# Loading the first two batches of a batched matmul one by one, with one load issued by a second engine

## The chip, the cores and the metric

The kernel runs on one core of a Trainium2 chip. The metric is device time in microseconds (us), of which the median of several executions is quoted. A profile also gives a *span*, from the first to the last recorded instruction. The span of this kernel is some 2 us shorter than its time.

## The reference

Sixteen independent products of 512 x 512 matrices in float32, with the left one transposed:

```python
a: (16, 512, 512) float32   # batch, k, m
b: (16, 512, 512) float32   # batch, k, n
out = np.matmul(a.transpose(0, 2, 1), b).astype(np.float32)
```

That is 33.55 MB to read and 16.78 MB to write.

## The kernel before

Batches are taken in eight pairs. One DMA loads both batches of a pair of `a` (2 MB), another those of `b`: batch 0 of the pair lies in partitions 0 to 63, batch 1 in 64 to 127, and each partition gets one contiguous run of 8 rows, 16 KB. There are four such float32 buffers. VectorE casts to bf16 in two halves (`v`), TensorE multiplies (two 64-row matmuls side by side, one for each batch), ScalarE copies PSUM to an output tile, and SyncE issues the DMAs. It issues all sixteen loads first and then the stores, which so stand behind the loads on one queue.

```python
for n in range(2 * pairs):                      # 16 loads, a and b in turn
    if n >= NX:                                 # NX = 4 buffers
        nc.sync.wait_ge(s_in, n - NX + 1)       # casts of load n - 4 done
    nc.sync.dma_start(x_ts[n % NX][:], in_v[n % 2][n // 2]).then_inc(s_x[n % NX], 16)
for i in range(pairs - 1):                      # the stores follow on the same queue
    nc.sync.wait_ge(s_out, i + 1)
    nc.sync.dma_start(out_v[i], o_ts[i % NO][:]).then_inc(s_o if i else s_o0, 16)
...
for i in range(pairs):                          # VectorE
    for v in range(V):
        if i and v == 0:
            nc.vector.wait_ge(s_v, G * i)
        if i and v == 1:
            nc.vector.wait_ge(s_mm, G * H * i)
        for n in (2 * i, 2 * i + 1):
            if v == 0:
                nc.vector.wait_ge(s_x[n % NX], 16 * (n // NX + 1))
            nc.vector.tensor_copy(...).then_inc(s_cast, 1)
            if v == V - 1:
                nc.vector.memset(dve_done[:, n:n + 1], 0.0).then_inc(s_in, 1)
```

## Time and profile before

| | before |
|---|---|
| time, median | 123.92 us (123.84 to 124.15, 4 runs) |
| span of the profile | 121.9 us |
| DMA engines busy | 97.6% |
| busiest compute engine | TensorE, 51% |
| DMA rate from 4 to 79 us (loads) | 430 to 434 GB/s |
| first cast, first matmul | 8.84 us, 15.19 us |

Each load and store ends with one small semaphore write on each of the 16 DMA engines, and the trace records them. The mean of the sixteen is called the *end* of a load in what follows. In the kernel before, ends in the middle of the run are 4.86 us apart.

### The profile page before, as it was taken

The page shows a single profiled execution, that of the slowest core. Times are in us where ns is not written, and L with a number is a line of the kernel's source. Part 1 is how long each engine was busy: PE and PEld are TensorE (multiplying, and loading weights), DVE is VectorE, ACT ScalarE, POOL GpSimd, SP SyncE. Part 2 cuts the span into 40 slices and gives each one's busy share as a digit, 9 for nine tenths or more (in the row PEclk, how much of TensorE's full clock was granted, in tenths as well). Part 3 has the DMA queues.
Part 4 walks back from the last instruction along what each step waited for, and adds up shares of the span by engine and source line. Part 5 has one row for each costly group of instructions (what it writes and reads, how often), then busy time and mean ns, then how long its engine had stood idle before and what let it go on. Part 6 is the DMA issues. An engine that isn't in the chain of part 4 may idle for free. (4 is left out here: it accounts for less than half of the span.)

```text
span 121.9 us, 1261 instructions
## 1 busy us (share of the span) xinstructions
PE 62.5 (51%) x512; PEld 35.8 (29%) x512; DVE 38.0 (31%) x48; ACT 31.8 (26%) x41; POOL 0.2 (0%) x4
## 2 busy tenths in 40 slices
PE   0000099989669749969919988946960000000000
PEld 0000044546246314536605645624630000000000
DVE  0003560784194092474356247419000000000000
ACT  4000000480920830190470075091083000000000
POOL 0000000000000000000000000000000000000000
PEclk9999999999999977999995899999999655555555
DMA  5899999999999999999999999999999999999994
GB/s 108 360 430 430 436 430 430 430 430 430 430 430 430 430 430 436 430 430 430 430 430 430 430 430 430 436 390 428 428 430 430 430 428 430 430 430 428 428 428 175
DMA packets 4480, 50.33 MB, mean 413 GB/s; under 512 B 384, under 2 KB 384, under 8 KB 384
## 3 DMA queue, kind: packets, MB, share of 16 engines
q1 hardware_dynamic: 4480, 50.33, 97.6%
HBM read 33.55 MB, written 16.78 MB: 413 GB/s over the span
## 5 line engine op out<-in xcount | busy, mean ns | idle before, releaser
L103 PE MATMUL ps<-bbf,abf 64*128 64x512 bf16 x512 | 62.5, 403 | 27.9 <-PEq L98 27.9
L103 PEld LDWEIGHTS ps<-bbf,abf 64*128 64x128 bf16 x512 | 35.8, 114 | 54.1 <-issue 37.8
L121 ACT COPY o<-ps 128x1024 f32<-128x1024 f32 x32 | 30.1, 1026 | 59.8 <-PE ps L103 59.8
L82 DVE CAST abf<-x 128x2048 bf16<-128x2048 f32 x16 | 19.6, 1224 | 26.6 <-PE ps L103 17.6
L82 DVE CAST bbf<-x 128x2048 bf16<-128x2048 f32 x16 | 19.6, 1225 | 20.8 <-DMA x<-in_b_dram 20.8
L126 ACT ACTIVATE done<-done 1x1 uint32<-1x1 uint32 x8 | 1.6, 196 | 0.0
L121 ACT ACT_TABLE_LOAD x1 | 1.3, 1283 | 0.9 <-SPq L64 0.9
L88 DVE MEMSET done<- 1x1 f32 x16 | 0.9, 59 | 0.0
L148 POOL MEMSET const-bfloat16-1.0<- 128x1 bf16 x1 | 0.1, 101 | 0.0
L148 POOL MEMSET const-uint8-127<- 128x1 uint8 x1 | 0.1, 101 | 0.0
L148 POOL MEMSET const-float32-0.0<- 128x1 f32 x1 | 0.1, 98 | 0.2 <-issue 0.2
L148 POOL MEMSET const-float32-1.0<- 128x1 f32 x1 | 0.1, 98 | 0.0
## 6 DMA issues: line engine op xcount, KB each, us to landing
x<-in_a_dram SPq DMA_DIRECT2D x8, 2048.0 KB, 12.1
x<-in_b_dram SPq DMA_DIRECT2D x8, 2048.0 KB, 15.9
out_dram<-o SPq DMA_DIRECT2D x8, 2048.0 KB, 30.8
```

What stands on the lines that cost most here:

```text
L82: nc.vector.tensor_copy(out=(bbf_ts if n % 2 else abf_ts)[v][:], in_=x_ts[n % NX][:, v * RV:(v + 1) * RV, :],).then_inc(s_cast, 1)
L88: nc.vector.memset(dve_done[:, n:n + 1], 0.0).then_inc(s_in, 1)
L103: mm = nc.tensor.matmul(ps_ts[g][h][:, t % 2, :], a_m[:, t], bbf_ts[v][rows, r, :], start=(v == 0 and r == 0), stop=(v == V - 1 and r == R ...
L121: ev = nc.scalar.copy(out=o_ts[i % NO][:, g, 2 * h:2 * h + 2, :], in_=ps_ts[g][h][:])
L126: nc.scalar.memzero(act_done[:, i:i + 1]).then_inc(s_out, 1)
L148: nc = _bacc.Bacc("TRN2", target_bir_lowering=False, num_devices=1)
```

## The change

First a and first b of pair 0 are loaded batch by batch, so that batch 0 (1 MB of `a`, 1 MB of `b`) is complete after half the bytes. Its `b` is issued by ScalarE at the same time as its `a` by SyncE. The aim is to let TensorE start earlier. Each partition then holds four rows of one batch (8 KB runs), and this pair uses 128-row matmuls. Both batches go through the same bf16 tiles, so VectorE must wait for the matmuls of batch 0 before it casts batch 1.

```diff
+    in0_v = [x.rearrange("batch (p r) m -> batch p r m", r=RV) for x in (a, b)]
...
-        for n in range(2 * pairs):
+        for u in range(G):
+            for j in range(2):
+                (nc.sync if u or j == 0 else nc.scalar).dma_start(
+                    x_ts[j][:, u * RV:(u + 1) * RV, :], in0_v[j][u]
+                ).then_inc(s_x[j] if u else s_f[j], 16)
+        for n in range(2, 2 * pairs):
...
+        for u in range(G):
+            if u:
+                nc.vector.wait_ge(s_mm, H)
+            for j, bf_ts in enumerate((abf_ts, bbf_ts)):
+                nc.vector.wait_ge(s_x[j] if u else s_f[j], 16)
+                nc.vector.tensor_copy(
+                    out=bf_ts[0][:], in_=x_ts[j][:, u * RV:(u + 1) * RV, :]
+                ).then_inc(s_cast, 1)
+                if u == G - 1:
+                    nc.vector.memset(dve_done[:, j:j + 1], 0.0).then_inc(s_in, 1)
... (VectorE: the old loop from pair 1 on, where pair 1 waits for all matmuls of pair 0;
     TensorE: a loop of two batches with 16 128-row matmuls each, then the old loop for 7 pairs;
     ScalarE: the four copies of pair 0 in batch order)
```

## The prediction

> **What bounds the kernel now.** I read the page first, parts 1 to 4, for which engine is full and when; then the stretches table, to find where the full resource is not full; then the timeline of the start and the queue's own waits, because that is where the change acts.
>
> ```profile
> PE 62.5 (51%) x512; PEld 35.8 (29%) x512; DVE 38.0 (31%) x48; ACT 31.8 (26%) x41; POOL 0.2 (0%) x4
> DMA  5899999999999999999999999999999999999994
> q1 hardware_dynamic: 4480, 50.33, 97.6%
> HBM read 33.55 MB, written 16.78 MB: 413 GB/s over the span
> ```
>
> No compute engine is above 51% of the span, while the 16 DMA engines are 97.6% busy and show a 9 in all but the first two slices and the last. The kernel is bound by moving 50.33 MB. The chain of work that ended last covers only 7% of the span for the same reason: it ends at the issue of the last store, and nearly everything else is transfers, which the chain does not price. What the change can win is therefore only DMA time that is not used at full rate. The stretches table says where that is (last two columns: DMA share and GB/s).
>
> ```profile
> 0.00:2.00 2.00, 0.00 (x0) 0.00 (x0) 0.00 (x0) 1.10 (x1) 0.20 (x4) 1.00 0.12 33
> 2.00:4.00 2.00, 0.00 (x0) 0.00 (x0) 0.00 (x0) 0.18 (x1) 0.00 (x0) 1.00 0.94 229
> 4.00:6.00 2.00, 0.00 (x0) 0.00 (x0) 0.00 (x0) 0.00 (x0) 0.00 (x0) 1.00 1.01 434
> 6.00:15.00 9.00, 0.00 (x0) 0.00 (x0) 2.56 (x3) 0.00 (x0) 0.00 (x0) 1.00 1.00 430
> 15.00:60.00 45.00, 38.35 (x312) 21.43 (x314) 22.44 (x29) 15.81 (x21) 0.00 (x0) 0.96 1.01 431
> 79.00:82.00 3.00, 1.64 (x16) 0.79 (x12) 0.21 (x1) 3.00 (x4) 0.00 (x0) 1.00 0.93 380
> 90.00:120.00 30.00, 0.42 (x4) 0.00 (x0) 0.00 (x0) 2.58 (x4) 0.00 (x0) 0.59 1.01 427
> 120.00:121.90 1.90, 0.00 (x0) 0.00 (x0) 0.00 (x0) 0.00 (x0) 0.00 (x0) 0.50 0.07 26
> ```
>
> From 4 us to 120 us the rate is 427 to 434 GB/s, except for a dip where loads give way to stores. Against 431, the deficits are 1.85 us in the first row (2.00 x (1 - 33/431)), 0.94 us in the second, 0.35 us at 79 to 82, and about 1.8 us at the end. These add up to 4.9 us, and 50.33 MB at 431 GB/s is 116.8 us; together 121.7 of the span's 121.9. Only the second row, 0.94 us, is something this change can act on: the first is the time before the first DMA can be issued and reach the engines, the last is the end of the program.
>
> The start itself, by the timeline:
>
> ```profile
> 0.94 0.39 SPq L68 DMA_DIRECT2D x<-in_a_dram  x1
> 1.39 0.42 SPq L68 DMA_DIRECT2D x<-in_b_dram  x1
> 8.84 1.23 DVE L82 CAST abf<-x 128x2048 bf16<-128x2048 f32 x1 [8.84 <-DMA x<-in_a_dram]
> 13.67 1.23 DVE L82 CAST bbf<-x 128x2048 bf16<-128x2048 f32 x1 [3.60 <-DMA x<-in_b_dram]
> 15.19 9.54 PE L103 MATMUL ps<-bbf,abf 64*128 64x512 bf16 x64 [15.19 <-PEq L98]
> 16.08 0.33 SPq L68 DMA_DIRECT2D x<-in_a_dram  x1
> 17.23 0.33 SPq L68 DMA_DIRECT2D x<-in_b_dram  x1
> 23.44 1.23 DVE L82 CAST bbf<-x 128x2048 bf16<-128x2048 f32 x1 [0.87 <-DMA x<-in_b_dram]
> ```
>
> The first a (2 MB) lands at 8.84, the first b at 13.67, TensorE starts at 15.19. That idle start looks like a loss, and it is what the change attacks. But the fifth load, the first that waits for a buffer, is issued at 16.08, and the last of the four loads before it lands at 23.44: the queue holds over 7 us of work when it gets more. Late compute never starves the transfers.
>
> **What the Trainium skill says.** "DMA: Bandwidth & Descriptors", section "Issuing engines are not separate DMA queues", says that DMAs from scalar, sync or gpsimd run on the same 16 engines and interleave, so issuing from several saves only the sequencer's issue time. The trace before uses one queue and cannot show the interleaving; it does show the issue time at stake, 0.39 to 0.42 us per load, against some 4.9 us for which a load keeps the engines busy. The same page, section "Queues, rings and completion order", says that each engine goes round-robin between the queues it has work for, packet by packet: so first a and first b should land together. No run here shows that yet. Section "Where 436 GB/s comes from" puts the ceiling at 435.2 GB/s; the trace agrees, with 427 to 434 in every full stretch, so there is no rate left to gain. "TensorE: Matmul & The Clock Gate", part 1, says that the array runs at half rate for about 3.4 us of work before it is warm. The trace shows the same in kind: 24 matmul instructions, 12 concurrent pairs, fill 15.16 to 20.24 us (5.05 us busy, 0.42 us a pair), then 42 fill 4.46 us (0.21 us a pair). It is longer than stated, and the measured 5.05 us is used below.
>
> **The change part by part.**
>
> 1. *Bytes.* Nothing is added or removed: the first 8 MB of loads are the same rows, only batch by batch. Cost 0.
>
> 2. *Packet size.* The first 4 MB go in 8 KB runs in place of 16 KB. In the trace's record of packets an engine starts a 16 KB load packet every 607 ns and an 8 KB store packet every 306.6 ns, so 8 KB costs 3 ns more per packet, if loads behave as stores. 4.19 MB is 512 packets, 32 per engine: 32 x 3 ns = +0.1 us. Two more DMAs mean 32 more semaphore writes, 9 ns each and two per engine: +0.02 us. All of this is on the path, as the DMA engines set the end.
>
> 3. *The second issuing queue.* The first b is issued by ScalarE at about 0.9 us instead of 1.39. The first packet only moves at 2.01 us, by when two loads have already been issued by SyncE alone. Each engine has 8 packets of a in front of it. So 0.45 us earlier brings bytes only if the engines are short of work between 2 and 4 us. There the first packets are slow (the packet record has 0.8 to 1.9 us for them, against 0.611 later), with work queued behind. If that is a first-access latency, a second queue may overlap it a little, or may not. I take -0.1 us of the 0.94, a choice; zero is as well founded. The ScalarE table load (1.28 us from 0.90) moves behind its issue; ScalarE has nothing to do until the first eviction at 23.03.
>
> 4. *Earlier compute.* First a and first b, 2 MB in all, land where 2 MB of a landed: about 8.8. Casts: 1.14 us apart, 1.23 us the last, then 0.26 us to TensorE (all as before): 8.84 + 1.14 + 1.23 + 0.26 = 11.5, 3.7 us earlier than before. This lies wholly beside the transfers and is worth 0.
>
> 5. *Delayed buffer release.* The new dependency: the casts of the second batch reuse the same bf16 tiles, so VectorE waits for all 16 matmuls of the first batch. Taking a 128-row matmul as one pair's time (an estimate; it streams the same 512 columns): 12 x 0.42 + 4 x 0.21 = 5.9 us, to 17.4. Cast of the second a ends 18.7, so the fifth load is issued near 18.8 instead of 16.08, the sixth near 20.0. The queue empties near 23.4, a margin of 4.6 us. Second batch: TensorE from about 20.1 to 23.5 warm, three casts, the seventh load near 27.2 against 26.07; the loads ahead of it land by 33.13 as before. From the b load that lands at 33 us on, VectorE waits for DMA as before and the old rhythm is back. Cost 0.
>
> 6. *The end.* The last store is issued at 92.7 and queued behind some 28 us of other stores (the queue's own waits show 27.8 us for it). Unchanged.
>
> Sum: +0.1 + 0.02 - 0.1 + 0 = about 0; against the 123.9 of before, I predict 123.9.
>
> **The rivals.** *First, starvation*: the delayed release in step 5 lets the queue run dry before the fifth load. Its support is the new wait, and a half-rate clock that could last longer. Against it is the margin: TensorE would have to take 4.6 us more for 16 matmuls that need at most 16 x 0.42 = 6.7 us even if none is at full pace. A dry queue would add its gap one for one; a 2 us gap would give 126. *Second, a faster ramp*: two queues at once fill the slow stretch from 2 to 4 us. At most 0.94 us, so 123.0; half of it gives 123.4. For it is that engines do start slowly; against it, that work was already queued behind the slow packets. *Third, a slower ramp*: a second queue and two tensors' rows interleaved make first accesses slower, or bringing ScalarE's queue into use costs something before the first packet. Some 0.3 to 0.5 us, giving 124.4. *Fourth, the intent as it reads*: earlier compute shortens the kernel by 3.7 us, to 120.2. The page speaks against it: the transfers alone need 116.8 us, with the start, the ramp and the end around them, and compute is done at 92.4.
>
> **Range and chances.** Three timed runs spread by 0.3 us. The packet cost is small and sure, the ramp is the one open term, from about -0.7 to +0.5. So 123.2 to 124.4. A change of 2% is 2.5 us: a gain of that size would need the whole ramp and most of the fixed start or end, a loss would need starvation. Faster 0.02, same 0.96, slower 0.02.
>
> **What would show each step right or wrong.** Step 2: packets rise from 4480 by 256 + 32 = 4768, the new 8 KB loads come every 306 to 307 ns per engine. Step 3: the stretch from 2 to 4 us is near 229 GB/s; 330 or more means the faster ramp. Step 4: the casts of first a and b begin near 8.8 and 10, matmuls near 11.5. Step 5: fifth load near 18.8, DMA row still all 9 from the third slice on; a lower digit near slice 8 means starvation. Step 6: last store issued near 92.7 and the last stretch unchanged. The prediction is wrong if the time moves by over 0.7 us, above all if the DMA row shows a gap that I have not named.

## The result, and the profile after

| | before | after |
|---|---|---|
| time, median | 123.92 us (4 runs) | 123.88 us (123.87 to 124.08, 4 runs) |
| ratio to before | | 0.9998, 95% interval 0.998 to 1.0015 |
| span of the profile | 121.9 us | 122.1 us |
| first cast, first matmul | 8.84, 15.19 us | 8.55, 11.21 us |
| fifth load of the old order issued | 16.08 us | 17.76 us |

Executions over 1.5% slower than the fastest of the same kernel are left out of the means. A ratio is from the runs of the same rounds, so not quite the ratio of the medians quoted. Those of the experiments mostly come out when each kernel's first, profiled run is left out.

The change is worth nothing. The page of the changed kernel, its DMA parts:

```profile
DMA  3999999999999999999999999989999999999993
DMA packets 4768, 50.33 MB, mean 412 GB/s; under 512 B 416, under 2 KB 416, under 8 KB 416
q1 hardware_dynamic: 4624, 49.28, 95.1%
q10 hardware_dynamic: 144, 1.05, 2.3%
HBM read 33.55 MB, written 16.78 MB: 412 GB/s over the span
```

The bytes are the same, the packets are 288 more, and the second queue (q10) carries just the one load. The row is about as full as before; its one 8 after the start is the slice from 79.4 to 82.4 us. The start, in the timeline of the changed kernel (start, duration, engine, line, operation; in brackets the idle time before it and what ended it):

```profile
0.90 0.39 ACTq L72 DMA_DIRECT2D x<-in_b_dram  x1
0.94 0.87 SPq L72 DMA_DIRECT2D x<-in_a_dram  x2
8.55 1.23 DVE L88 CAST abf<-x 128x2048 bf16<-128x2048 f32 x1 [8.55 <-DMA x<-in_a_dram]
9.69 1.22 DVE L88 CAST bbf<-x 128x2048 bf16<-128x2048 f32 x1
11.21 5.24 PE L122 MATMUL ps<-bbf,abf 128*128 128x512 bf16 x16 [11.21 <-PEq L120]
16.48 1.23 DVE L88 CAST abf<-x 128x2048 bf16<-128x2048 f32 x1 [5.58 <-PE ps L122]
17.76 0.33 SPq L78 DMA_DIRECT2D x<-in_a_dram  x1
```

TensorE does start 4.0 us earlier. Then VectorE waits 5.58 us for TensorE, the new wait, and the first buffer is handed back 1.7 us later than before. Neither shows in the time. What does show a difference is the stretches table (last two columns: DMA share, GB/s), in two of its rows:

```profile
2.00:4.00 2.00, 0.00 (x0) 0.00 (x0) 0.00 (x0) 0.61 (x1) 0.00 (x0) 1.00 0.68 238
79.00:82.00 3.00, 2.61 (x26) 1.26 (x20) 0.49 (x2) 2.09 (x3) 0.00 (x0) 1.00 0.92 360
```

The start, called the *ramp* from here because the engines come up to full rate in it, is a little better than before (238 against 229 GB/s). The *hand-over* from loads to stores is worse (360 against 380). By the semaphore writes, the last load but one ends 0.15 us earlier than before (75.90 against 76.05 us), but the last load then takes 5.31 us in place of 4.99, where 4.86 is full pace. From the end of the last load to the end of the last store it is 39.2 us in both, so what had been won at the start was given back inside the last load, near 80 us. There is only one profile of the kernel before, so how far its own hand-over varies is not known. The experiments ask whether the loss is scatter, and what causes it.

One more point can be read off. On two queues first a and first b do land together, as the prediction expected: by the sixteen semaphore writes of each, they end at 7.78 and 7.77 us. In sp_only below, on one queue, they end at 5.15 and 7.61 us.

### The profile page after: what moved, and what is told of

The parts are those of the page before. It is cut to its first block, busy times and chain, and to the rows that moved or that the text cites. A ratio compares the mean times of both kernels' runs of the same rounds, so it can differ in the third digit from the quotient of the medians.

```text
span 122.1 us, 1205 instructions
## 1 busy us (share of the span) xinstructions
PE 61.6 (50%) x480; PEld 35.2 (29%) x480; DVE 37.8 (31%) x48; ACT 32.2 (26%) x41; POOL 0.2 (0%) x4
## 2 busy tenths in 40 slices
DMA packets 4768, 50.33 MB, mean 412 GB/s; under 512 B 416, under 2 KB 416, under 8 KB 416
## 5 line engine op out<-in xcount | busy, mean ns | idle before, releaser
L142 PE MATMUL ps<-bbf,abf 64*128 64x512 bf16 x448 | 52.7, 393 | 15.1 <-PEq L137 15.1
L142 PEld LDWEIGHTS ps<-bbf,abf 64*128 64x128 bf16 x448 | 31.4, 112 | 36.4 <-issue 21.6
L122 PE MATMUL ps<-bbf,abf 128*128 128x512 bf16 x32 | 8.9, 440 | 13.9 <-PEq L120 13.9
L122 PEld LDWEIGHTS ps<-bbf,abf 128*128 128x128 bf16 x32 | 3.7, 122 | 18.6 <-issue 16.5
```

The lines of the kernel that those rows point to most:

```text
L122: mm = nc.tensor.matmul(ps_ts[0][h][:, t % 2, :], a_m[:, r, t], bbf_ts[0][:, r, :], start=(r == 0), stop=(r == RV - 1),)
L142: mm = nc.tensor.matmul(ps_ts[g][h][:, t % 2, :], a_m[:, t], bbf_ts[v][rows, r, :], start=(v == 0 and r == 0), stop=(v == V - 1 and r == R ...
```

## The experiments

Theory: the kernel is bound by transfers, so that earlier compute is worth nothing, and the time moves only with the DMA engines' start, their hand-over, and any gap in between. Rivals: the start of compute is on the path; the second queue or the 8 KB runs have a cost or a gain of their own; the later release starves the queue.

### after_again: the changed kernel once more

> The changed kernel once more, unaltered, with more rounds and a second profile. My theory (the kernel is bound by its transfers, the change moves only compute and the first packets): ratio to the kernel before 0.998 to 1.0015 again, 123.7 to 124.1 us; the stretch from 2 to 4 us near 238 GB/s as in its first profile. The first profile also shows a slower hand-over from loads to stores (360 GB/s at 79 to 82 us, before had 380): if the change causes that, the new profile shows 355 to 365 again; if it is scatter from run to run, it may come anywhere from 360 to 385.

Measured: 123.9 us (5 runs), ratio 1.0000, interval 0.9987 to 1.0013. In the second profile the stretch from 2 to 4 us moved 254 GB/s and that from 79 to 82 us 336. The last load but one ended at 75.87 us and the last load took 5.22 us. The hand-over is slow again, so it is not one unlucky profile. But 336 lies below both ranges that were expected (355 to 365, and 360 to 385): its size varies more than either reading allowed.

The span was 122.1 us in both profiles, 0.2 us above that of before, while the times are equal. Time less span is 1.96 to 1.98 us for the kernel before and 1.73 to 1.78 us for the changed one. So 0.2 us more inside the span is offset by 0.2 us less outside it, a part of the time that no profile records. Why is open; the next kernels show both values, without a link to their first loads (two kernels that add only one wait to the kernel before have 1.7 as well).

### sp_only and act_whole: the two halves of the change at the start

sp_only is the changed kernel with everything on SyncE:

```diff
-                (nc.sync if u or j == 0 else nc.scalar).dma_start(
+                nc.sync.dma_start(
```

> The changed kernel with the first load of b issued by SyncE as well, so that only the batchwise 8 KB loads are left of the change. Theory (issue time is worth nothing with work queued): within 0.2 us of the changed kernel. Rival (the second queue fills the ramp): the stretch from 2 to 4 us falls from 238 GB/s to 229 or lower and the time rises by up to 0.2 us. First a and first b land near 8.6 and 8.8 in either case.

act_whole is the kernel before with one load moved:

```diff
-            nc.sync.dma_start(x_ts[n % NX][:], in_v[n % 2][n // 2])...
+            (nc.scalar if n == 1 else nc.sync).dma_start(x_ts[n % NX][:], in_v[n % 2][n // 2])...
```

> The kernel before with only one thing changed: the whole first load of b (2 MB in 16 KB runs) is issued by ScalarE. Theory: no change beyond 0.2 us, 123.7 to 124.1; first a and b land together near 13.5 instead of 8.84 and 13.67, TensorE starts near 16 instead of 15.2, fifth load near 17.3, all of it free. Rival (the ramp gain is from the second queue): the stretch from 2 to 4 us rises above 229 GB/s as in the changed kernel and the time is 0.1 to 0.3 us lower than before, without the cost of the 8 KB runs.

Measured: sp_only 124.02 us (6 runs), ratio 1.0005 (0.9992 to 1.0017); act_whole 124.32 us (5 runs), ratio 1.0021 (1.0008 to 1.0034). Neither is faster. But both start clearly better than before, and better than the changed kernel. sp_only casts first a at 5.86 us and starts its matmuls at 9.79, another 1.4 us earlier than the changed kernel, and has nothing from it. The stretches table of sp_only:

```profile
2.00:4.00 2.00, 0.00 (x0) 0.00 (x0) 0.00 (x0) 0.18 (x1) 0.00 (x0) 1.00 0.74 295
79.00:82.00 3.00, 1.22 (x12) 0.52 (x8) 0.00 (x0) 3.00 (x4) 0.00 (x0) 1.00 0.89 273
```

And of act_whole:

```profile
2.00:4.00 2.00, 0.00 (x0) 0.00 (x0) 0.00 (x0) 0.60 (x1) 0.00 (x0) 1.00 0.85 303
77.00:79.00 2.00, 2.00 (x22) 1.34 (x20) 0.76 (x1) 0.77 (x1) 0.00 (x0) 1.00 1.29 401
79.00:82.00 3.00, 0.95 (x10) 0.32 (x6) 0.00 (x0) 3.00 (x5) 0.00 (x0) 1.00 0.73 262
```

So act_whole has 303 GB/s at the start in place of 229, and then 262 at the hand-over in place of 380. A share of 1.29 at 401 GB/s means that each packet takes longer: the table counts a packet whole in the stretch in which it starts, so long packets that run over the edge bring the share above 1. (They do not run side by side: there are never more than 17 under way on the 16 engines.) The packet records have 16 KB packets of up to 1396 ns there, against 611. They are slow *before* the first store packet moves (81.4 us). Of the last load's 128 packets, those over 650 ns number 9 in the kernel before, 24 and 25 in the two profiles of the changed one, 45 in sp_only and 44 in act_whole. All profiles, by the packet records (first column: MB moved in the first 6 us, each packet's bytes spread evenly over its duration):

| kernel | MB by 6 us | last load but one ends, us | last load takes, us |
|---|---|---|---|
| before | 1.243 | 76.05 | 4.99 |
| changed, two profiles | 1.338, 1.347 | 75.90, 75.87 | 5.31, 5.22 |
| sp_only | 1.410 | 75.73 | 5.96 |
| act_whole | 1.454 | 75.60 | 6.00 |
| all8k (below) | 1.316 | 76.42 | 4.90 |

Both halves of the change speed up the ramp, by 0.3 us (batchwise 8 KB loads, one queue) and 0.45 us (second queue, 16 KB runs) at the last load but one. Kernels below with the same first loads put the first at 0.2 us (timed_sp) and the second at 0.40 to 0.49 us (late_stores, reversed, timed_act). Together they gave 0.15 to 0.18 us. Then the last load gives back all of it and more. sp_only's profile fell on its slowest run (124.47 us); its other runs have probably lost less. The expectations fared badly. Theory: sp_only's time is within 0.2 us of the changed kernel as said, but act_whole's is above the 123.7 to 124.1 us expected, and sp_only's ramp and landings are not as said. Rival: in act_whole the second queue does fill the ramp, but the time rose where it should have fallen; in sp_only the ramp got faster where it should have gone back to 229 GB/s. Where the theory was right about the time, it was so only because something else took the gain away.

### all8k: the cost of 8 KB runs, eight times over

All loads in 8 KB runs, compute untouched, so that the result is wrong:

```diff
-    in_v = [x.rearrange("(pair g) (q r) m -> pair (g q) r m", g=G, r=R) for x in (a, b)]
+    in_v = [x.rearrange("(pair g) (p r) m -> pair p g (r m)", g=G, r=RV) for x in (a, b)]
```

> The kernel before with every load in 8 KB runs (two per partition), the compute untouched, so that its result is wrong on purpose: both batches of a pair are mixed. It makes the suspected packet cost of the change eight times as large. Theory (3 ns more per 8 KB packet): 33.55 MB are 4096 packets, 256 per engine, 256 x 3 ns = +0.77 us, so 124.7 (124.4 to 124.9). Rival (load packets of 8 KB cost nothing extra): 123.9. Rival (a first access per run is costly): over 125.5.

Measured: 124.16 us (6 runs), ratio 1.0013 (0.9999 to 1.0027), so only some 0.16 us, and the expectation fell. The packet cost itself is there: load ends are 4.90 us apart in place of 4.86, 0.038 us for 2 MB or 0.6 us for sixteen loads. But by 6 us it had moved 0.073 MB more than before (0.17 us at 431 GB/s), and its last load was at its full pace of 4.90 us, where before lost 0.13. For the two loads' worth of 8 KB runs in the change, the cost is 2 x 0.038 = 0.08 us.

### wait_x2 and wait_x3: compute started later

The kernel before with one line more ahead of VectorE's loop, for the third load or the fourth:

```diff
+        nc.vector.wait_ge(s_x[2], 16)      # wait_x3: s_x[3]
         for i in range(pairs):
             for v in range(V):
```

> The kernel before, with VectorE made to wait for the third load before its first cast. Compute starts some 5 us later than before (casts near 18.5, TensorE near 20), and the fifth load is issued near 22.1 instead of 16.08, when the queue has about 1 us of work left. Theory (transfers bound; the start of compute is worth nothing until the queue runs dry): +0 to +0.6 us, as an issue needs about 1 us to its first packet. Rival (start of compute is on the path): +4 to +5 us, 128 to 129.

> The kernel before, with VectorE made to wait for the fourth load before its first cast: compute starts some 10 us later, the fifth load is issued near 27.0, its first packet near 28, and the queue is empty from about 23. Theory (starvation costs its gap one for one, and only its gap): about 4.9 us of empty DMA near 23 to 28 us, time 128.3 to 129.0. Rival (start of compute is on the path): +9 to +10 us, 133 to 134. Rival (slack elsewhere absorbs a gap): under 126.

Measured: wait_x2 125.89 us over its four fast runs (a fifth, slow one took 127.92), ratio 1.0143 (1.0121 to 1.0165). wait_x3 has two fast runs, 130.71 and 132.54 us, which is 5.5% and 7.0% above before (two slow ones took 134.07 and 133.04). Both cost more than the theory said, and wait_x3 lies between its range and the rival's. The DMA row and the issue of the fifth load in the profile of wait_x2:

```profile
DMA  5899999799999999999999999999999999999992
...
21.98 0.33 SPq L68 DMA_DIRECT2D x<-in_a_dram  x1
```

The 7 is a gap in the transfers at about 22 us. The fifth load ends 1.42 us later than before (28.85 against 27.43 us), though first compute is 5.9 us later (matmuls from 21.09). So the start of compute is not what costs; the gap is. I had put the end of the queued work at 23.4 us, the last engine's landing. The first engine is dry at 22.2, and an issue takes about 1 us to its first packet (0.94 to 1.96 us at the start, 21.98 to 22.96 here). In wait_x3 no packet starts between 22.45 and 27.87 us, a gap of 5.4 us (4.9 expected), but the fifth load ends 6.39 us late: the restart pays for a slow ramp again. Starvation costs its gap plus a new ramp, which my "one for one" left out. Both also slow the last load (5.49 and 5.42 us). The two fast times of wait_x3 are 1.8 us apart; that scatter is not explained.

### late_stores: no store behind the last loads

act_whole, whose hand-over is worst, with the stores held back until the last load has landed:

```diff
+        nc.sync.wait_ge(s_x[3], 16 * (2 * pairs // NX))
         for i in range(pairs - 1):
             nc.sync.wait_ge(s_out, i + 1)
```

> act_whole with one wait more: SyncE issues the first store only when the last load has landed, so that no store stands in the queue behind the last loads. In act_whole the last load's packets slowed from 611 to as much as 1396 ns between 77.8 and 80.4 us, before any store packet moved, and the last load ended at 82.0 instead of about 80.9. Theory A (stores queued behind the loads slow the last load): the packets stay at 611 ns, the last load ends near 80.9, then the engines stand idle for about 1.1 us (an issue to its first packet), time 124.3 to 124.8. Theory B (it is the last load itself, or its time): slow packets stay, the last load ends near 82, plus the idle 1.1 us, time 125.2 to 125.8.

Measured: 124.95 us (4 runs). The last load takes 4.86 us, full pace, and not one of its packets is slow; it ends at 80.51 us, against 81.60 in act_whole. Then the engines stand idle until the first store, issued at 81.46, moves at 82.38:

```profile
77.00:79.00 2.00, 2.00 (x22) 1.35 (x20) 1.21 (x1) 0.33 (x1) 0.00 (x0) 1.00 0.97 418
79.00:82.00 3.00, 1.40 (x14) 0.62 (x10) 0.54 (x1) 3.00 (x4) 0.00 (x0) 1.00 0.42 180
```

The mechanism of theory A holds: with stores standing in the queue since 65.6 us the last load is slow, before any of them moves data, and without them it is not. The time is above A's range, because the idle stretch was 1.9 us and not 1.1: the wait is for the last of the sixteen engines (81.16 us), and the issue comes 0.3 us after that.

### reversed: another place in memory

act_whole with pairs taken from last to first (loads and stores alike: `pairs - 1 - n // 2` and `pairs - 1 - i` as indices).

> act_whole with the pairs of batches taken from the last to the first, so that the last load reads the start of the tensors and the first load their end. If the slow packets belong to a place in memory, they leave the last load; if they belong to the hand-over from loads to stores, they stay between 77 and 81 us and the time stays within 0.4 us of act_whole (124.0 to 124.6).

Measured: 124.23 us (4 runs); the last load takes 5.68 us, with packets of up to 1218 ns between 77.7 and 81 us. The slow packets stay with the hand-over, not with an address.

### both_ends: 8 KB runs at the hand-over

sp_only with the last pair in 8 KB runs, and its matmuls batch by batch as the first pair's:

```diff
+            if n // 2 == pairs - 1:
+                nc.sync.dma_start(
+                    x_ts[n % NX][:].rearrange("p (g r) m -> p g (r m)", g=G), in8_v[n % 2][n // 2]
+                ).then_inc(s_x[n % NX], 16)
...  (in8_v is the view of all8k; an unrolled batchwise tail on TensorE, and its copies in batch order on ScalarE)
```

> sp_only (first pair loaded batch by batch in 8 KB runs, all from SyncE) with the last pair in 8 KB runs and batch by batch too, result correct. all8k showed no slow packet at the hand-over, sp_only and act_whole lost 0.8 to 1.2 us there. If the 8 KB packets at the hand-over are what spares all8k the loss: lead of about 0.4 us at 6 us, less 0.1 us for each of the two 8 KB pairs, hand-over loss near 0 instead of 0.3 in the kernel before: 123.4 to 123.7, the best of all. If not: 123.9 to 124.3 as sp_only.

Measured: 124.68 us (124.25 to 125.35, 6 runs), ratio 1.0054, result correct. The last load takes 5.40 us, where 4.90 is full pace for 8 KB, so the shorter runs do not spare it. The time is above both expected ranges, so the expectation fell, and why all8k is spared is open. Beyond that, time less span grew to 2.26 us on average and scatters more; which part of the unrolled tail does that was not tried.

### timed_act, timed_sp, timed_before: stores issued just in time

If stores must not stand behind the loads for long, and must not come late either, they want to be issued some 2 us before the loads end. The first half of the seventh pair's results is complete near there (after three quarters of its matmuls; the expectation below says it loosely):

```diff
+        nc.sync.wait_ge(s_mm, G * H * (pairs - 2) + G)
         for i in range(pairs - 1):
             nc.sync.wait_ge(s_out, i + 1)
```

> act_whole with the first store held back until the first half of the seventh pair's matmuls is done (near 78.4 us), so that its first packets can move near 79.4, about 1.5 us before the last load ends, neither 13 us early as in act_whole nor 1.2 us late as in late_stores. Theory (stores standing behind the loads slow the last load, in proportion to the time that they stand there): hand-over loss 0.3 us or less in place of 1.2, the ramp's lead of about 0.5 us is kept, time 123.3 to 123.7, faster than both kernels. If a short time behind the loads slows them as much: 124.1 to 124.4.

> The same wait in sp_only. Theory: hand-over loss 0.3 us or less in place of 0.5 to 1.0, time 123.4 to 123.8. Otherwise 123.9 to 124.3.

> The same wait in the kernel before, whose hand-over loss is only 0.3 us in its profile. Theory: 0.0 to 0.3 us less, 123.6 to 123.9. If the held-back stores cost an idle gap at the hand-over instead: 124.0 to 124.5.

Measured in the same rounds, before at 123.87 us (11 runs):

| kernel | time, median | ratio (95%) | last load but one ends | last load takes |
|---|---|---|---|---|
| timed_act | 123.40 us, 5 runs | 0.9962 (0.9949 to 0.9975) | 75.56 | 4.86 |
| timed_sp | 123.19 us, 6 runs | 0.9951 (0.9932 to 0.9969) | 75.85 | 4.86 |
| timed_before | 123.75 us, 6 runs | 0.9992 (0.998 to 1.0005) | 76.03 | 4.86 |

The intervals of the first two lie below 1. In all three the last load is at full pace, with no packet over 650 ns. timed_act, the same rows as act_whole above, and its issue of the stores:

```profile
2.00:4.00 2.00, 0.00 (x0) 0.00 (x0) 0.00 (x0) 0.60 (x1) 0.00 (x0) 1.00 0.95 336
77.00:79.00 2.00, 2.00 (x22) 1.34 (x20) 0.76 (x1) 0.78 (x1) 0.00 (x0) 1.00 0.99 426
79.00:82.00 3.00, 0.95 (x10) 0.32 (x6) 0.95 (x1) 3.00 (x5) 0.00 (x0) 1.00 0.96 410
...
78.25 5.95 SPq L72 DMA_DIRECT2D out_dram<-o  x6
```

410 GB/s at the hand-over where act_whole had 262. act_whole and timed_act differ in one wait and by 0.9 us (124.32 and 123.40), or 0.7 us by their ratios, each to the kernel before of its own rounds (they ran on different chips). The ramp's gain is real, and it reaches the end of the kernel once the hand-over no longer takes it. timed_before shows that without a better ramp the wait alone is worth about 0.1 us, within its interval. The changed kernel itself was not run with this wait. timed_sp has the lowest median. It is below timed_act although its ramp is slower; time less span is 1.74 us in it and 1.99 in timed_act, which is the difference seen in the changed kernel too. Its profile fell on a slower run (123.68 us) in which the stores were issued only at 80.14 us, with 0.6 us lost to an idle gap (its stores end 39.8 us after its last load, 39.2 us in timed_act): the wait hangs on TensorE's pace, and TensorE ran part of that pair at half rate.

What these runs do not tell apart is the time that stores stand behind the loads, how many do, and a full queue. In the timed kernels stores also stand behind the last load, for some 2 us, and do not slow it. In the kernel before they have stood there for some 15 us, since 66.3 us, and the issue of one of them lasts 9.07 us (from 69.76 us), where timed_act issues six in 5.95 us. That a full queue is what slows the loads would be a guess; no run tests it.

## Why the prediction was right

The time (123.88 against 123.9) and the verdict were right, and the main reason too. That the number fits to 0.02 us is in part luck: two effects near the two ends of the loads, neither of which the sum had at its size, and 0.2 us outside the span cancelled.

- **The bound** held. Compute 4.0 us earlier in the changed kernel, 5.4 us earlier in sp_only, and 5.9 us later in wait_x2 moved the time only as far as transfers moved. The fourth rival, the intent as it reads, is out.
- **Bytes and packets** (steps 1 and 2) held: 4768 packets as predicted. The cost of 8 KB runs was 0.08 us by all8k's pace, where the step had 0.1.
- **The second issuing queue** (step 3) was mis-sized and misattributed. It gave -0.1 us to the second queue, as a choice. The lead before the last load, with the 8 KB cost already in it, was 0.15 to 0.18 us; the second queue alone gives 0.40 to 0.49, the batchwise 8 KB loads alone 0.2 to 0.3. Why both together give less was not found. So of the second rival, the faster ramp, a small part came true, and the third, the slower ramp, did not. (The first packet moves at 1.96 us, not at 2.01 as the step has it; nothing hangs on that.)
- **Earlier compute** (step 4): casts at 8.55 and 9.69 us and matmuls from 11.21 (8.8, 10 and 11.5 predicted), worth nothing.
- **Delayed release** (step 5): the fifth load at 17.76 us, 18.8 predicted. The term that was most off is the half-rate stretch of the matmuls, taken as 5.05 us; here it was some 3.4 us (eight of sixteen matmuls, 11.21 to about 14.56 us). (The row of granted clock reads 1.00 in both of these stretches; the half rate is seen only in the matmuls' pace.) No starvation, as said. But the margin of 4.6 us was too generous: here the first engine has done its queued loads at 22.05 us, and with 1.0 us from issue to first packet the margin is 22.05 - 1.0 - 17.76 = 3.3 us.
- **The end** (step 6) is the step that failed. It read "Unchanged" because the last store is issued near 92.7 (92.87 measured) behind other stores. What was missed lies ahead of those: the hand-over, where the last load took 5.2 to 5.3 us instead of 4.99. The prediction listed it as a 0.35 us deficit "at 79 to 82" and then said that only the start could change. The late_stores and timed kernels show that it comes from stores queued early behind the last load (in act_whole, sp_only and the kernel before; the changed kernel was not run with the stores held back).

So the sum of "about 0" came out as about -0.15 us at the ramp, +0.2 to +0.3 us at the hand-over, a little more from engines that end further apart, and -0.2 us outside the span. What stays open: what happens inside the DMA engines when stores stand behind loads, why the same stores cost 0.13 us in one kernel and 1.1 us in another, and the 0.2 us outside the span.

## What to carry to other kernels

When the DMA engines are full throughout, starting compute earlier is worth nothing; look instead for the stretches where they are not at full rate, here the ramp, the hand-over from loads to stores, and any gap. Small gains at the start can be lost later, so follow the lead through the run (the end of each load) before calling a change worthless. Where loads and stores share one queue, try issuing the stores shortly before the loads end. Here about 2 us before was right (78.25 us, with the last load ending at 80.42); 15 us before slowed the last load, and after its end left the engines idle for 1.9 us. For act_whole's first loads that one wait turned a 0.2% loss into a 0.4% gain; for the kernel before it was worth 0.1%, which is within its interval.

## What the Trainium skill lacked or had wrong

- "DMA: Bandwidth & Descriptors", section "Where 436 GB/s comes from", says that HBM to SBUF transfers are bound by the HBM side at some 358 GB/s. One core alone loaded from HBM at 430 to 434 GB/s for 75 us here. (The same page gives 425 for a large load, so it is only the sentence on which side binds that does not fit a core that runs alone.)
- The same page, "Issuing engines are not separate DMA queues", says that a second issuing engine only saves issue time. The runs do not show this wrong, but they show that it can be worth something although a 2 MB load has been issued already: with one first load moved to ScalarE, 1.454 MB were moved in the first 6 us in place of 1.243, a lead of 0.45 us that lasted to the last load. The issue came 0.49 us earlier (0.90 us in place of 1.39), so the lead may be no more than the issue time saved. But the changed kernel saved as much and led by 0.15 to 0.18 us. The cause is open.
- None of the DMA and HBM pages that I read for this says that stores queued behind loads slow those loads. The last 2 MB load took 4.99 to 6.00 us with 16 KB runs and stores queued early, and 4.86 us in all four kernels that held them back. With 8 KB runs throughout and stores queued early it was spared too (4.90 us).
- "TensorE: Matmul & The Clock Gate", part 1, gives about 3.4 us of half-rate work and says that it varies from run to run. The trace agrees in the changed kernel (3.4 us) and shows 5.05 us in the kernel before.
